# Squares moved behind the last products, weight casts and evacuations spread over later steps, and SP's transfers in written order, in a two-layer decoder trunk

## The chip, the cores and the metric

The kernel runs on one core of a Trainium2 chip. The core has a matrix engine (PE, with its weight loads listed as PEld), three engines for elementwise work (DVE, ACT, POOL) and a queue engine (SP) that issues transfers between HBM and the on-chip memory; here nearly all transfers are issued on SP. The metric is the device time of one execution in microseconds. The throttle on PE's clock is seen in the profile as the granted clock, 1.00 being full speed.

## The reference

The input x is 1024 positions by 1024 features, in float32. Two layers follow each other, each a token mixer and a feed-forward network with residual adds, with an RMS norm ahead of each part:

```
h = x
h = h + rg_lru_block(rms_norm(h, mix_norm[0]), ...)      # layer 0: recurrent mixer
h = h + swiglu_ffn(rms_norm(h, ffn_norm[0]), ...)        # d_ff = 2816
h = h + stick_breaking_attention(rms_norm(h, mix_norm[1]), w_qkv, w_o)   # layer 1, 16 heads of 64
h = h + swiglu_ffn(rms_norm(h, ffn_norm[1]), ...)
return rms_norm(h, final_norm)
```

The stick-breaking attention takes, for each query t and each earlier position s, sigmoid(z) at s times the product of sigmoid(-z) over the positions between s and t, where z is the scaled product of query and key; these weights multiply the values. The product of the sigmoids is a running product along the keys, so it is a scan.

## The kernel before

**Products.** Every float32 product is made of three matrix products in a reduced format (`mm3`, L140 to L143): the operands are split into a high and a low part, and high by high, high by low and low by high are added in PSUM. A split costs a cast (high part, usually on ACT) and a subtraction (low part, usually on DVE). Weights come as `raw` (a 128x1024 tile of 512 KB, `load_raw`, L114, from three buffers) and become `whi` and `wlo`. The activations are kept transposed: `h[d][n]` is the row block d of 8 (128 features) and the half n of 2 (512 positions); `xh[d][n]` and `xl[d][n]` are the two parts of h times the norm's gain. The normalising factor of each position is applied after the products, by a multiply with `rbc[n]`, so the products can begin before the statistics are known.

**End of layer 0.** The feed-forward network does its output product over 13 visits (`VISITS`), each for two row blocks d and d + 4, in seven products of halves (`ORDER`); in the last two visits rows 3, 7, 0 and 4 become final. When a row half has had its last add, `finished` (L1035) stores it (L1040, on SP), makes xh and xl (`prep`, L215 on ACT and L216 on DVE), and adds its square to the sum of squares (`squares`: L211 on ACT into a buffer, one for each n, L212 on DVE into `rbc[n]`). The weights of the first projection are loaded, cast and subtracted inside the last visit.

**Attention.** The program `qkv_steps(q)` makes, for the head pair q (0 to 7), the three projections Q, K and V (`which` 0, 1, 2), each in two halves n of eight `mm3` each over the rows k = 0 to 7, into one of two PSUM banks (`qk_ps`). It gives control back after each `mm3`, so a pair has 48 steps. At the start of each projection it loads the weights of the next one and casts them at once (`next_weights`: L1307, one 128x1024 cast on ACT); the two halves of the subtraction (L1309, DVE) are put into a list, `later`, of which the main loop takes one item a turn. At the end of a half the bank is evacuated: `t` (L1337, DVE, the multiply with `rbc[n]`), and in the same step, for Q and K, the cast `qh_` (L1346, ACT), the subtraction `ql_` (L1347, DVE) and the moves to the tiles that the scores read (L1348, on SP, 4 for a Q half and 8 for a K half); `qh_` and `ql_` have one buffer each, `t` has two. For V the half is transposed later (`v_turn`, `vt_ps`, put into a list `late`).

The main loop goes over 192 units of 16 heads. A turn does: the scores of a chunk (`z_part`, L1388 and L1389, PE, two PSUM banks `z_ps`); the transposes of weights two units ahead (`t_part`, L1426, PE) and their split `th`, `tl` (L1435 ACT, L1436 DVE); the two sigmoids of the scores, F (L1408) and w (L1409), on ACT, the scan over F (L1412 or L1414, DVE) and the multiply of w by F (L1415, POOL); one item of `later`; two steps of the fill, which is the projections of the next pair; and the product with the values (`av_part`, L1447, L1448). The scores run eight units ahead of the products with the values (`LEAD`). Before the loop, a prologue runs all 32 steps of Q and K of pair 0, with the statistics in between (`stats`: `st_ps` L201, `ms` L203, then a chain of small operations; `broadcast_r`: `rb_ps` L189, copied to `rbc`, L196), from the fifth step on.

After the last pair, the outputs of the heads, which had been stored to HBM in `od`, are brought back into xh and xl (L1495, L1496), the banks of the projections are closed, and the fill goes on with the output projection's first products (`ob`).

**What sets the order.** `tc.manual_schedule` keeps, on the engines it names, the order in which the program is written; operations of other engines are placed by the planner, which may issue a load long before the place where it is written. In the attention PE, ACT, DVE and POOL are named, SP is not. Each engine works through its instructions in order, so an instruction that waits holds up those behind it.

## Time and profile before

| | |
|---|---|
| time, median of three runs | 2208.43 us (2207.1 to 2210.01) |
| the profiled execution's own time | 2209.81 us |
| its span, first to last instruction | 2207.9 us |
| mean granted clock of PE | 0.994 |
| PE busy | 2176.5 us (99%) |
| DVE busy | 1709.9 us (77%) |
| ACT busy | 1150.2 us (52%) |
| load of attention weights, 512 KB, issue to landing | 3.8 us |

A line of the timeline gives the start of an instruction in us from the start of the span, its duration, the engine, the line of the kernel, the operation, what it writes and reads, and in brackets how long the engine sat idle before it and which engine's result ended that. A row with a count such as x8 is several instructions in a run. A waits line gives the engine and instruction that waited, what it waited for, the total, how often, and the longest. A busy PE is not a PE at its full clock: at clock 0.50 each matmul takes twice as long and still counts as busy.

### The profile page before, as it was taken

The numbers are of one execution on the slowest core, as the hardware profiler recorded it, in microseconds if no ns is written. First come the engines' busy times: TensorE is split into PE (matmuls) and PEld (weight loads), VectorE is DVE, ScalarE is ACT, GpSimd is POOL, SyncE is SP. The second block draws the span as 40 slices with busy tenths as digits, with TensorE's granted clock in tenths as the row PEclk, the third lists the DMA queues.
The fourth block names the chain that finished last, engine by engine and source line by source line (L and its number), as shares of the span: only waits on it lengthen the run. The fifth ranks groups of instructions, "written<-read, shape, count | busy, mean of one in ns | idle before, by whom it ended". The sixth has DMA issues, their size and how long they took to land.

```text
span 2207.9 us, 28478 instructions
## 1 busy us (share of the span) xinstructions
PE 2176.5 (99%) x10120; PEld 1805.7 (82%) x10120; DVE 1709.9 (77%) x2383; ACT 1150.2 (52%) x2007; POOL 287.2 (13%) x379
## 2 busy tenths in 40 slices
PE   7999999999999999999999999989999999999998
PEld 6888888888888888878888888878888888888887
DVE  6887778767777887878888888876876777788876
ACT  5577435343444544546666666653533444454556
POOL 2222020000000000003334333321000000000002
PEclk9999999999999999999999999989999999999999
DMA  7111412334444764444333333532133444467442
GB/s 230 48 48 39 134 39 72 102 123 158 143 149 134 261 209 122 148 136 98 89 94 96 105 87 104 177 128 70 39 110 124 148 148 133 154 225 234 137 152 86
DMA packets 298702, 277.72 MB, mean 126 GB/s; under 512 B 16312, under 2 KB 215104, under 8 KB 298560
## 3 DMA queue, kind: packets, MB, share of 16 engines
q1 hardware_dynamic: 298544, 275.91, 40.1%
q8 instruction: 79, 1.29, 0.2%
q14 instruction: 63, 0.52, 0.1%
q10 hardware_dynamic: 16, 0.00, 0.0%
HBM read 175.71 MB, written 74.97 MB: 114 GB/s over the span
## 4 chain that ended last, share of the span: by engine, by line
PE 88%; DVE 6%; ACT 3%; DMA 1%; issue 1%; SPq 1%; DVEq 0%; ACTq 0%
PE p_ps L143 18%; PE p_ps L141 18%; PE p_ps L142 18%; PE qk_ps L143 3%; PE qk_ps L141 3%; PE qk_ps L142 3%; PE wt_ps L1426 3%; PE ob_ps L142 2%; PE ob_ps L141 2%; PE ob_ps L143 2%; PE a_ps L143 2%; PE a_ps L142 2%; PE a_ps L141 2%; PE z_ps L1388 1%; DVE F L1414 1%; PE z_ps L1389 1%
## 5 line engine op out<-in xcount | busy, mean ns | idle before, releaser
L1415 POOL TENSOR_TENSOR w<-w,F 128x128 f32<-128x128 f32 (+1 forms) x192 | 183.7, 957 | 311.1 <-DVE F L1412 159.0
L143 PE MATMUL p_ps<-vh,wcl 128*128 128x512 f32 x524 | 204.2, 390 | 0.5 <-DVE wcl L682 0.5
L143 PE MATMUL p_ps<-vh,wbl 128*128 128x512 f32 x524 | 204.4, 390 | 0.3 <-DVE wbl L672 0.2
L143 PE MATMUL p_ps<-vh,wal 128*128 128x512 f32 x524 | 204.1, 389 | 0.1
L141 PE MATMUL p_ps<-vh,wbh 128*128 128x512 f32 x524 | 204.2, 390 | 0.0
L141 PE MATMUL p_ps<-vh,wch 128*128 128x512 f32 x524 | 204.1, 389 | 0.0
L142 PE MATMUL p_ps<-vl,wbh 128*128 128x512 f32 x524 | 203.9, 389 | 0.0
L142 PE MATMUL p_ps<-vl,wch 128*128 128x512 f32 x524 | 203.9, 389 | 0.0
L141 PE MATMUL p_ps<-vh,wah 128*128 128x512 f32 x524 | 203.9, 389 | 0.0
L142 PE MATMUL p_ps<-vl,wah 128*128 128x512 f32 x524 | 203.9, 389 | 0.0
L668 ACT CAST wbh<-sb 128x1024 fp32r<-128x1024 f32 (+2 forms) x69 | 69.6, 1009 | 193.7 <-DVE sb L652 193.6
L212 POOL TENSOR_TENSOR acc<-acc,rbc 128x512 f32<-128x512 f32 x30 | 40.4, 1348 | 773.6 <-ACT rbc L211 773.6
L1436 DVE TENSOR_TENSOR tl<-wt_ps,th 128x512 fp32r<-128x512 f32 x192 | 106.0, 552 | 39.2 <-ACT th L1435 37.1
L1435 ACT CAST th<-wt_ps 128x512 fp32r<-128x512 f32 x192 | 92.5, 482 | 83.1 <-PE wt_ps L1426 82.0
L141 PE MATMUL qk_ps<-vh,whi 128*128 128x512 f32 x264 | 118.6, 449 | 0.7 <-ACT vh L215 0.7
L143 PEld LDWEIGHTS p_ps<-vh,wbl 128*128 128x128 f32 x524 | 98.3, 188 | 22.3 <-DVE wbl L672 2.0
L143 PEld LDWEIGHTS p_ps<-vh,wcl 128*128 128x128 f32 x524 | 98.4, 188 | 21.9 <-DVE wcl L682 1.6
L143 PEld LDWEIGHTS p_ps<-vh,wal 128*128 128x128 f32 x524 | 98.4, 188 | 21.3 <-DVE wal L663 1.0
L142 PEld LDWEIGHTS p_ps<-vl,wah 128*128 128x128 f32 x524 | 98.4, 188 | 20.6
L142 PEld LDWEIGHTS p_ps<-vl,wch 128*128 128x128 f32 x524 | 98.4, 188 | 20.5
L142 PEld LDWEIGHTS p_ps<-vl,wbh 128*128 128x128 f32 x524 | 98.4, 188 | 20.5
L141 PEld LDWEIGHTS p_ps<-vh,wbh 128*128 128x128 f32 x524 | 98.4, 188 | 20.3 <-ACT ta L1053 0.2
(400 smaller groups left out, 5851.2 us busy)
## 6 DMA issues: line engine op xcount, KB each, us to landing
raw<-in_ffn_w_in SPq DMA_DIRECT2D x88, 512.0 KB, 3.8
vl<-pd SPq DMA_DIRECT2D x128, 256.0 KB, 3.6
pd<-U SPq DMA_DIRECT2D x90, 256.0 KB, 2.3
raw<-in_ffn_w_out SPq DMA_DIRECT2D x56, 256.0 KB, 3.9
raw<-in_attn_w_qkv SPq DMA_DIRECT2D x24, 512.0 KB, 3.8
raw<-in_lru_w_in SPq DMA_DIRECT2D x16, 512.0 KB, 4.1
acc<-pd SPq DMA_DIRECT2D x28, 256.0 KB, 2.6
pph<-rbc SPq DMA_DIRECT2D x28, 256.0 KB, 2.5
```

The lines of the kernel that those rows point to most:

```text
L141: nc.tensor.matmul(ps, lhsT=wh, rhs=mh, start=first, stop=False, **kw)
L142: nc.tensor.matmul(ps, lhsT=wh, rhs=ml, start=False, stop=False, **kw)
L143: nc.tensor.matmul(ps, lhsT=wl, rhs=mh, start=False, stop=last, **kw)
L212: (eng or nc.gpsimd).tensor_add(acc[n], acc[n], sq)
L668: nc.scalar.copy(self.full(self.wb), self.full(self.sb))
L1388: nc.tensor.matmul(ps[:, 0 : c1 - c0], lhsT=lhsT, rhs=KH[q][hx][:, c0:c1], start=True, stop=False)
L1389: nc.tensor.matmul(ps[:, 0 : c1 - c0], lhsT=lhsT, rhs=KL[q][hx][:, c0:c1], start=False, stop=True)
L1414: nc.vector.tensor_tensor_scan(rev, rev, rev, first, op0=ALU.mult, op1=ALU.bypass)
L1415: nc.gpsimd.tensor_mul(wt, wt, F[:, 1 : n + 1])
L1426: nc.tensor.transpose(tp[:, c : c + P], W[q, hx, j, kb // 4][:, (kb % 4) * P : (kb % 4 + 1) * P], ident)
L1435: nc.scalar.copy(th[:, q0:], tp[:, q0:])
L1436: nc.vector.tensor_sub(tl[:, q0:], tp[:, q0:], f32(th)[:, q0:])
```

## The change

- The squares of the four row blocks that become final in the last two visits (d = 0, 3, 4, 7, both halves) are left out of `finished`, and are done after the last products, first all of n = 0, then all of n = 1.
- `next_weights` does its work in three items of `later` in place of one cast at once and two items: the first half of the cast; the first half of the subtraction and the second half of the cast; the second half of the subtraction. Each is taken in a turn of its own.
- The first projection, Q of pair 0, takes its rows in the order 1, 5, 2, 6, 3, 7, 0, 4.
- The evacuation becomes a program of its own (`evacuate`): `t` is made in the step that ends the half, the rest (cast, subtraction, moves, or the entry of `v_turn` into `late`) a step later. For Q of pair 0 the whole of it is done at set places of the prologue.
- The prologue has 34 steps in place of 32; the statistics stand behind its steps 9 and 12, the broadcasts behind 14 and 18, the evacuations of Q behind 16 and 19 (`between`).
- The output's copies back from `od` are issued partly in V of the last pair (n = 0, pairs 0 to 5), the rest at the end; two empty steps before the first products of `ob` go.
- SP is named in the attention's `manual_schedule`, so the transfers are issued in the order written.

```diff
@@ -1029,7 +1029,8 @@
                     a, b = (ta, tb), GT[0] if final else held[0]
                 return dict(zip((0, 2, 3, 4), (*a, half(b, 0), half(b, 1))))
 
-            begun_sq = set()
+
+            begun_sq, last_sq = set(), []
             done = []
 
             def finished(d, n):
@@ -1039,7 +1040,10 @@
                 else:
                     nc.sync.dma_start(hd[d][n], h[d][n])
                     prep(h, d, n, gnext)
-                    squares(h, d, n, acc, rbc, V, first=n not in begun_sq)
+                    if d in (VISITS[-1][0], VISITS[-2][0], VISITS[-1][0] + HK, VISITS[-2][0] + HK):
+                        last_sq.append((d, n))
+                    else:
+                        squares(h, d, n, acc, rbc, V, first=n not in begun_sq)
                 begun_sq.add(n)
 
 
@@ -1196,6 +1200,8 @@
                         open_last()
             for dn in done:
                 finished(*dn)
+            for d, n in sorted(last_sq, key=lambda t: t[1]):
+                squares(h, d, n, acc, rbc, V, first=False)
             if final:
                 finish(h, nw, R, pp, (*GT, *UT))
         gs.close()
@@ -1300,21 +1306,29 @@
         wq = {(0, 0): wq0[0]}
 
 
-        late, later = [], []
+        late, later, waiting = [], [], []
+
+        def bring_back(*which):
+            for q, n in which:
+                nc.sync.dma_start(f32(xh[q][n]), od[q, n][0])
+                nc.sync.dma_start(f32(xl[q][n]), od[q, n][1])
 
         def next_weights(raw):
             hi, lo = wtile("whi"), wtile("wlo")
-            nc.scalar.copy(hi, raw)
-            for i in range(NH):
-                later.append(lambda c=half(hi, i), a=half(lo, i), b=half(raw, i): nc.vector.tensor_sub(a, b, f32(c)))
+            part_hi = lambda i: nc.scalar.copy(half(hi, i), half(raw, i))
+            part_lo = lambda i: nc.vector.tensor_sub(half(lo, i), half(raw, i), f32(half(hi, i)))
+
+            def second():
+                part_lo(0)
+                part_hi(1)
+
+            later.extend((lambda: part_hi(0), second, lambda: part_lo(1)))
             k3 = lambda t: t.rearrange("p (k c) -> p k c", k=ND)
             return k3(hi), k3(lo)
 
 
 
         def qkv_steps(q):
-            full = lambda tag: [ap.tile([P, S], F32R, tag=tag, name=tag, bufs=4) for _ in range(2)]
-            VV[q] = ap.tile([P, NT, 2, P], F32R, tag="v", name="v", bufs=2)
             for which in range(3):
                 w = wq.pop((q, which))
                 nx = (q, which + 1) if which < 2 else (q + 1, 0)
@@ -1325,51 +1339,67 @@
                     mix[0].w[mix[0].order[0]] = next_weights(mix[0].raw.pop(0))
                     mix[0].load(1)
                     mix[0].load(2)
+
+                ks = (1, 5, 2, 6, 3, 7, 0, 4) if (q, which) == (0, 0) else range(ND)
                 for n in range(NH):
                     ps = psQ.tile([P, NB], F32, tag="qk", name="qk_ps")
-                    for k in range(ND):
-                        mm3(ps, w[0][:, k], w[1][:, k], xh[k][n], xl[k][n], k == 0, k == ND - 1)
-                        if k == 3 and late:
+                    for i, k in enumerate(ks):
+                        mm3(ps, w[0][:, k], w[1][:, k], xh[k][n], xl[k][n], i == 0, i == ND - 1)
+                        if i == 3 and late:
                             late.pop()()
-                        if k < ND - 1:
+                        if i < ND - 1:
                             yield
-                    t = ap.tile([P, NB], F32, tag="t", name="t", bufs=2)
-                    nc.vector.tensor_mul(t, ps, rbc[n])
-                    cs = slice(n * NB, (n + 1) * NB)
-                    if which == 0 and n == 0:
-                        Q[q] = full("q")
-                    if which == 1 and n == 0:
-                        KH[q], KL[q] = full("kh"), full("kl")
-                    if which < 2:
-                        th = ap.tile([P, NB], F32R, tag="qh_", name="qh_", bufs=1)
-                        tl = ap.tile([P, NB], F32R, tag="ql_", name="ql_", bufs=1)
-                        nc.scalar.copy(th, t)
-                        nc.vector.tensor_sub(tl, t, f32(th))
-                        move = lambda dst, p0, src, p1: nc.sync.dma_start(f32(dst)[p0, cs], f32(src)[p1])
-                        for hx, (a, b) in enumerate(((top, bot), (bot, top))):
-                            if which == 0:
-                                move(Q[q][hx], a, th, a)
-                                move(Q[q][hx], b, tl, a)
-                            else:
-                                for dst, src in ((KH[q][hx], th), (KL[q][hx], tl)):
-                                    move(dst, top, src, a)
-                                    move(dst, bot, src, a)
+                    ev = evacuate(q, which, n, ps)
+                    if (q, which) == (0, 0):
+                        waiting.append(ev)
+                        yield
                     else:
-
-                        def v_turn(n=n, t=t):
-                            tp = psQ.tile([P, NB], F32, tag="qk", name="vt_ps")
-                            for i in range(4):
-                                nc.tensor.transpose(tp[:, i * P : (i + 1) * P], t[:, i * P : (i + 1) * P], ident)
-                            src = tp.rearrange("p (b h c) -> p b h c", b=4, h=2)
-                            bs = slice(4 * n, 4 * n + 4)
-                            for hx in range(2):
-                                nc.scalar.copy(VV[q][:, bs, hx, 0:HD], src[:, :, hx])
-                                nc.vector.tensor_sub(
-                                    VV[q][:, bs, hx, HD:P], src[:, :, hx], f32(VV[q])[:, bs, hx, 0:HD]
-                                )
-
-                        late.append(v_turn)
-                    yield
+                        next(ev)
+                        yield
+                        next(ev, None)
+
+
+        def evacuate(q, which, n, ps):
+            full = lambda tag: [ap.tile([P, S], F32R, tag=tag, name=tag, bufs=4) for _ in range(2)]
+            t = ap.tile([P, NB], F32, tag="t", name="t", bufs=2)
+            nc.vector.tensor_mul(t, ps, rbc[n])
+            yield
+            cs = slice(n * NB, (n + 1) * NB)
+            if which == 0 and n == 0:
+                Q[q] = full("q")
+            if which == 1 and n == 0:
+                KH[q], KL[q] = full("kh"), full("kl")
+            if which < 2:
+                th = ap.tile([P, NB], F32R, tag="qh_", name="qh_", bufs=1)
+                tl = ap.tile([P, NB], F32R, tag="ql_", name="ql_", bufs=1)
+                nc.scalar.copy(th, t)
+                nc.vector.tensor_sub(tl, t, f32(th))
+                move = lambda dst, p0, src, p1: nc.sync.dma_start(f32(dst)[p0, cs], f32(src)[p1])
+                for hx, (a, b) in enumerate(((top, bot), (bot, top))):
+                    if which == 0:
+                        move(Q[q][hx], a, th, a)
+                        move(Q[q][hx], b, tl, a)
+                    else:
+                        for dst, src in ((KH[q][hx], th), (KL[q][hx], tl)):
+                            move(dst, top, src, a)
+                            move(dst, bot, src, a)
+                return
+            if n == 0:
+                VV[q] = ap.tile([P, NT, 2, P], F32R, tag="v", name="v", bufs=2)
+
+            def v_turn():
+                tp = psQ.tile([P, NB], F32, tag="qk", name="vt_ps")
+                for i in range(4):
+                    nc.tensor.transpose(tp[:, i * P : (i + 1) * P], t[:, i * P : (i + 1) * P], ident)
+                src = tp.rearrange("p (b h c) -> p b h c", b=4, h=2)
+                bs = slice(4 * n, 4 * n + 4)
+                for hx in range(2):
+                    nc.scalar.copy(VV[q][:, bs, hx, 0:HD], src[:, :, hx])
+                    nc.vector.tensor_sub(VV[q][:, bs, hx, HD:P], src[:, :, hx], f32(VV[q])[:, bs, hx, 0:HD])
+
+            late.append(v_turn)
+            if q == NP - 1 and n == 0:
+                bring_back(*((p, 0) for p in range(NP - 2)))
 
 
         W = {}
@@ -1478,22 +1508,11 @@
         units = [u for q, hx in heads for u in unit_list(q, hx)]
         LEAD = 8
 
-
-        def stats_steps():
-            for n in range(NH):
-                stats(rbc[n], psO, "o", n)
-                for _ in range(ND - (1 if n else 6)):
-                    yield
-                broadcast_r(psO, "o", n)
-                yield
-
         def all_fill():
             yield from first
             for q in range(1, NP):
                 yield from qkv_steps(q)
-            for q, n in od:
-                nc.sync.dma_start(f32(xh[q][n]), od[q, n][0])
-                nc.sync.dma_start(f32(xl[q][n]), od[q, n][1])
+            bring_back((NP - 2, 0), *((p, 1) for p in range(NP - 2)))
             yield
             yield
             late.pop()()
@@ -1502,8 +1521,6 @@
             po = pos.enter_context(tc.tile_pool(name="fpo", bufs=1, space=PSUM, side="right", reuse_waits="tile"))
             ob = po.tile([P, S], F32, name="ob")
             mix.append(ob)
-            for _ in range(2):
-                yield
             for i, d in enumerate(mix[0].order[:2]):
                 w = mix[0].w[d]
                 for k in range(ND - 1):
@@ -1514,15 +1531,23 @@
         fill = all_fill()
         ready = {}
         E = mybir.EngineType
-        with tc.manual_schedule(engines={E.PE, E.Activation, E.DVE, E.Pool}):
-            sts, first = stats_steps(), qkv_steps(0)
-
-
-            for i in range(2 * ND * NH):
-                if i >= 5:
-                    next(sts, None)
+        with tc.manual_schedule(engines={E.PE, E.Activation, E.DVE, E.Pool, E.SP}):
+
+
+            first = qkv_steps(0)
+            between = {
+                9: lambda: stats(rbc[0], psO, "o", 0),
+                12: lambda: stats(rbc[1], psO, "o", 1),
+                14: lambda: broadcast_r(psO, "o", 0),
+                16: lambda: [*waiting[0]],
+                18: lambda: broadcast_r(psO, "o", 1),
+                19: lambda: [*waiting[1]],
+            }
+            for i in range(1, 2 * ND * NH + 3):
                 next(first)
-                if i >= 5 and later:
+                if i in between:
+                    between[i]()
+                if i > 4 and later:
                     later.pop(0)()
             for u in range(-LEAD, len(units)):
                 c = u + LEAD
```

## The prediction

> **What bounds the kernel now.** I read the page first (busy shares, chain), then the waits of PE and of the queue SP, then two stretches in the timeline: the end of layer 0 with the start of attention, and one period of attention.
>
> ```profile
> span 2207.9 us, 28478 instructions
> PE 2176.5 (99%) x10120; PEld 1805.7 (82%) x10120; DVE 1709.9 (77%) x2383; ACT 1150.2 (52%) x2007; POOL 287.2 (13%) x379
> raw<-in_attn_w_qkv SPq DMA_DIRECT2D x24, 512.0 KB, 3.8
> ```
>
> ```profile
> PE ob L141 <- issue: 3.9, 1, 3.9
> PE z_ps L1388 <- ACT w L1409: 2.5, 7, 0.4
> ```
>
> ```profile
> SPq L114 <- DVE wlo L1309: 104.3, 22, 17.5
> ```
>
> PE is busy 99% of the span, so a gain can only be idle PE time or time at half clock, and any new PE wait is paid in full. In the waits (total, times, longest), the largest single idle stretch of attention is the 3.9 us before `ob`; the waits of z for ACT come to 2.5 us over seven times. The third fence matters most: loads of the attention weights (L114) wait 104.3 us for a free buffer (released by `wlo`). They run as far ahead as three buffers allow, and land (3.8 us) long before their cast.
>
> **End of layer 0** (start, duration, engine; the bracket is the idle time before and what ended it):
>
> ```profile
> 923.83 0.39 PE L143 MATMUL p_ps<-vh,wcl 128*128 128x512 f32 x1
> ...
> 925.87 0.39 PE L143 MATMUL p_ps<-vh,wal 128*128 128x512 f32 x1
> ...
> 959.27 0.50 PE L143 MATMUL p_ps<-vh,wcl 128*128 128x512 f32 x1 [0.53 <-DVE wcl L682]
> 962.26 0.50 PE L141 MATMUL p_ps<-vh,wd 128*128 128x512 f32 x1 [0.42 <-ACT ta L1053]
> 968.77 0.51 PE L141 MATMUL qk_ps<-vh,whi 128*128 128x512 f32 x1 [0.66 <-ACT vh L215]
> 969.95 0.50 PE L142 MATMUL qk_ps<-vl,whi 128*128 128x512 f32 x1 [0.67 <-DVE vl L216]
> ```
>
> ```profile
> 968.00:971.30 3.30, 1.98 (x11) 1.24 (x10) 2.49 (x4) 2.53 (x4) 0.17 (x1) 1.00 0.70 240
> 971.30:974.70 3.40, 3.40 (x11) 2.82 (x11) 2.20 (x8) 0.20 (x1) 0.52 (x3) 0.50 0.00 0
> 1439.80:1445.70 5.90, 5.90 (x20) 5.02 (x21) 4.67 (x5) 3.51 (x9) 1.09 (x1) 0.50 0.71 202
> ```
>
> In the second fence (length, PE busy, PEld, DVE, ACT, POOL, granted clock), PE was idle 3.30 − 1.98 = 1.3 us up to 971.30, and the next 3.40 us ran at clock 0.50, a loss of 1.7 us. After the 3.91 us of `ob`, 5.9 us ran at 0.50: 3.0 us lost.
>
> Moving the last eight squares behind the products frees ACT and DVE for the work that PE waits for, and the new row order (rows finished early first) hides `prep`. Undisturbed matmuls of this size start every 0.227 us (nine starts from 923.83 to 925.87). The four waits show 0.53 + 0.42 + 0.66 + 0.67 = 2.3 us of idle time; by the starts around them against 0.227 each, they lost 0.80 + 0.70 + 0.82 + 1.05 = 3.4. With the 1.7 of half clock: −5.1 us.
>
> What becomes late is the statistics, which need the squares:
>
> ```profile
> 965.03 0.62 ACT L211 ACTIVATE acc<-h 128x512 f32<-128x512 f32 x1
> 969.80 0.68 DVE L212 TENSOR_TENSOR rbc<-rbc,acc 128x512 f32<-128x512 f32 x1
> 970.54 1.18 PE L201 MATMUL st_ps<-ones,rbc 128*128 128x1 f32 x8
> ```
>
> The squares of one half share one buffer, so each takes ACT 0.62, then DVE 0.68, and some 0.07 of handover: 1.38 us. Four of n = 0 take 5.5 us after the last `prep`. `st_ps` of n = 0 stands behind nine products (0.68 us each, three matmuls of 0.227), which started while `prep` of the last rows was still to do: by hand it waits 1.75 us, the second one 2.55 (three products cover 2.0 of a chain that ends 4.6 later), and the second projection 0.25 for the scale. Added: 4.55 us, and half clock between nothing and one stretch of 3.4 us; I take the 1.7 lost in the row above. Net +1.1 us (−5.1 if the new waits are all covered, to +2.9).
>
> **Start of attention.** SP's order is now the written one: the load of the third weights stands behind the four moves of the first Q half, and each evacuation's rest comes one step later.
>
> ```profile
> 976.38 0.69 DVE L1337 TENSOR_TENSOR t<-qk_ps,rbc 128x512 f32<-128x512 f32 x1
> 977.84 0.53 SPq L1348 DMA_DIRECT2D q<-qh__7618  x1
> 979.69 0.59 SPq L1348 DMA_DIRECT2D q<-ql__7619  x1
> 990.46 1.10 SPq L1348 DMA_DIRECT2D kh<-qh__7720  x2
> 994.70 0.36 PE L1389 MATMUL z_ps<-kl,q 128*128 128x256 f32 x1
> 995.97 0.62 ACT L1346 CAST qh__7759<-t 128x512 fp32r<-128x512 f32 x1 [5.53 <-DMA kh<-qh__7720]
> 996.61 1.28 ACT L1408 ACT_TABLE_LOAD   x1
> 998.40 0.44 PE L1388 MATMUL z_ps<-kh,q 128*128 128x384 f32 x1 [0.32 <-ACT w L1409]
> ```
>
> Count from the end of the first `t` (T). First move at T + 0.8 (977.84 − 977.07), fourth done at T + 3.2; the load issues at 3.3, lands at 7.1 (3.8). DVE's order is `wlo` of these weights before the second `t`: half a `whi` (0.53, see 1112.21 to 1112.74 below), half a `wlo` (0.66), `t` (0.69): T + 9.04. The second K half's products, needing that bank, were ready at T + 6.5: a stall of 2.55 us. `th` has one buffer, and waits for the DMA that reads it (5.53 in the row): second Q half moved at T + 9.8 to 12.25, its readers landed at 13.45, first K half moved from 14.1; z(0) needs the first of these landed, 4.2 us later as before (990.46 to 994.70): T + 18.3, while PE gets there at 15.9: 2.35 us. `th` of the second K half follows 5.5 us after the first move (990.46 to 995.97): 19.6; its eight moves end 5.6 later (0.65 from `th` to the first, as 1112.21 to 1112.86 below, and 4.96, as 1112.86 to 1117.82): 25.1. Only then is the first load of pair 1 issued; landed 28.95; two halves of cast 30.1; the table load, which stood before that cast, now stands behind it: 31.4; F and w of z(0): 31.9. z(2) needs that, and PE is ready at 21.75: 10.15 us. Sum 15.05, less the z waits of this place (0.8), plus half clock after the long stall (3.4 to 6.8 us of it: 2.5 lost) and after the two others (1.7): +18.5 us (12 to 21).
>
> **Each later pair.** One period is 60.4 us for 24 steps of the loop, two projection steps each. The rows around the second Q half and the second K half of pair 1:
>
> ```profile
> 1089.71 0.61 ACT L1409 ACTIVATE w<-z_ps 128x512 f32<-128x512 f32 x1
> 1094.05 0.61 ACT L1435 CAST th<-wt_ps 128x512 fp32r<-128x512 f32 x1
> 1094.81 0.41 ACT L1409 ACTIVATE w<-z_ps 128x256 f32<-128x256 f32 x1
> 1109.77 0.60 ACT L1409 ACTIVATE w<-z_ps 128x512 f32<-128x512 f32 x1
> 1112.21 0.62 ACT L1346 CAST qh__9181<-t 128x512 fp32r<-128x512 f32 x1 [1.84 <-DVE t L1337]
> 1112.74 0.37 ACT L1435 CAST th<-wt_ps 128x256 fp32r<-128x256 f32 x1
> 1115.03 0.26 ACT L1435 CAST th<-wt_ps 128x128 fp32r<-128x128 f32 x1
> 1115.46 0.39 ACT L1409 ACTIVATE w<-z_ps 128x256 f32<-128x256 f32 x1
> ```
>
> ```profile
> 1092.43 0.46 SPq L1348 DMA_DIRECT2D q<-qh__8931  x1
> 1094.32 0.59 SPq L1348 DMA_DIRECT2D q<-ql__8932  x1
> 1112.86 1.10 SPq L1348 DMA_DIRECT2D kh<-qh__9181  x2
> 1116.57 1.25 SPq L1348 DMA_DIRECT2D kl<-ql__9182  x2
> ```
>
> ```profile
> 1097.84 0.39 PE L1388 MATMUL z_ps<-kh,q 128*128 128x512 f32 x1
> 1117.03 0.39 PE L1388 MATMUL z_ps<-kh,q 128*128 128x512 f32 x1
> ```
>
> The delayed rest is a gain: ACT need not sit 1.84 us for `t`, and six of the seven z waits on w (some 0.5 us each with the drain) go, one a pair. But the load behind a rest is now issued after that rest's moves, and its cast stands on ACT one loop step later, ahead of the next `th`, F and w. K case: the half's cast starts when the last w ends (1110.37), eight moves run 1111.05 to 1116.1 (as long as 1112.86 to 1117.82), the load lands at 1119.9. ACT reaches that of the weights at 1111.6 (1110.37, that half's 0.53 and 0.7 for `th`, F and w of the next step) and stands until then, two z buffers and `th` two units ahead cover some steps, then PE stops: cast 0.53, then `th`, F and w (0.82, from 1115.03 to 1115.85) give 1121.25 for the z wanted at 1117.03: 4.2 us. Q case: the cast of the half starts at 1090.3 (1089.71 + 0.60), four moves 1090.95 to 1093.4, landed 1097.3; 0.53 and 1.17 (`th` to the end of w, 1094.05 to 1095.22) give 1099.0 for the z wanted at 1097.84: 1.2 us. The third load of a pair stands behind no move and runs ahead. Half clock after 4.2 us of stall is priced by the nearest row, 3.91 us of idle: 3.0 lost (0 to 3.4); after 1.2 us by 1.3 us idle followed by 1.7, against the seven waits of 0.4 us followed by none: 0.5 (0 to 1.7). A pair costs 4.2 + 1.2 + 3.0 + 0.5 − 0.5 = +8.4; seven pairs (the last one's K case waits for the first weights of `w_o` in the same way): +58.6 (25 to 73).
>
> **End of attention.** The two empty steps before `ob` go and the copies back to `xh` for n = 0 are issued earlier, so `vt_ps` and `ob` come back to back; but `ob` takes the banks that V's copies read, and waits for these as now: nothing, +1 for one more unit behind the fill where DVE is late (−4 to +2).
>
> Sum: 1.1 + 18.5 + 58.6 + 1 = +79 on the profiled run's 2209.81 (span 2207.9 and 1.9 around it), 2289; that run stands 1.4 over the median of 2208.43, so 2287.5.
>
> [...]
>
> **Rivals.**
> [...] Chance 0.17.
> (2) The loads of the pairs are covered: z's two buffers, `th` two units ahead and ACT (52% busy) catch up. For it: 5.4 us of slack between 1111.6 and 1117.03. Against: the load needs 8.3. It decides at 5.4 us from ACT's arrival to landing, that is, if the moves are issued in 2 us in place of 5. Then only the start pays: 1 + 18.5 + 1 − 3.7 = +17: 2225. Chance 0.13.
> (3) Faster: SP's loads are not late anywhere, since the moves' data come earlier by the whole delay of a rest; then −5.1 at the end of layer 0, −0.8 at z(2), −3.7 in the pairs and 2 of the 4.55 added: 2208 − 8 = 2200. It decides when the load of pair 1 lands before z(2) is wanted, 10 us sooner than my chain. Chance 0.05.
> (4) Worse: DVE (77%), idle while ACT stands, does not catch up after ACT's stop and PE stops a second time for `tl`, 2 to 4 us a pair: 2300 to 2315. Chance 0.12.
> (5) The loads keep their lead and the squares take back what the waits give: same. Chance 0.04.
>
> **Numbers.** The forecast itself (2268 to 2300) has 0.49. The range goes from 2222, just under the time of (2), to 2310: it holds 0.49, 0.17, some 0.10 of (2) and 0.07 of (4). About 0.2% (4.4 us) is what can be told from no change: faster 0.05, same 0.04, slower 0.91.
>
> **What would show it.** In the changed kernel: some 14 waits of `whi` on ACT for the DMA of `raw`, 3 to 8 us each; PE waits of z for w of about 4 us once and 1 us once a period; about 68 us a period; clock below 1 some 3 to 7 us after each; no waits for `vh` and `vl` at 968. If `raw` on SP still lies a projection ahead of its moves, or ACT's casts don't wait, the prediction is wrong.

## The result and the profile after

The changed kernel takes 2302.09 us (median of four runs, 2296.0 to 2303.02), the kernel before beside it 2208.98 us. The ratio is 1.042 (95% interval 1.040 to 1.044): 93 us slower. The forecast was 2287 us, within 2222 to 2310; the time lies just above the forecast's own band of 2268 to 2300.

The page of the kernel after: span, busy shares, and the chain of work that ended last, by engine.

```profile
span 2300.9 us, 28495 instructions
PE 2204.2 (96%) x10120; PEld 1823.5 (79%) x10120; DVE 1713.2 (74%) x2383; ACT 1154.0 (50%) x2031; POOL 295.2 (13%) x379
PE 83%; DVE 6%; DMA 4%; ACT 3%; SPq 2%; issue 2%; DVEq 0%; ACTq 0%
```

PE executes the same 10120 instructions, but is now idle 4% of the span, and DMA stands on the chain with 4%. The waits of the kernel after (total, times, longest) name the place:

```profile
ACT whi L1318 <- DMA raw<-in_attn_w_qkv: 111.1, 15, 9.9
PE z_ps L1418 <- ACT w L1439: 60.4, 15, 11.2
ACT whi L1318 <- DMA raw<-in_attn_w_o: 9.1, 1, 9.1
PE ob L141 <- issue: 5.2, 1, 5.2
```

ACT stands 16 times, 7.5 us on average, at the cast of weights that have not landed. PE waits 15 times for the w that is queued on ACT behind such a cast. In the kernel before that wait of PE came to 2.5 us.

I cut both traces at the same four pieces of work: the first product of the first projection, the first projection product of pair 1, the last projection product, and the last product with the values. The windows of the kernel before, then of the kernel after (from, to, length, then PE busy, PEld, DVE, ACT, POOL, and the granted clock):

```profile
963.75:1010.70 46.95, 45.17 (x215) 36.57 (x213) 29.05 (x51) 19.45 (x37) 6.62 (x17) 0.96 0.50 129
1010.70:1431.61 420.91, 418.70 (x2237) 352.24 (x2236) 355.57 (x516) 278.01 (x677) 166.10 (x280) 1.00 0.38 103
1431.61:1478.78 47.17, 40.55 (x200) 33.48 (x199) 38.03 (x50) 29.80 (x73) 16.41 (x25) 0.86 0.31 105
```

```profile
960.42:1029.69 69.27, 51.11 (x211) 40.34 (x209) 30.20 (x54) 21.88 (x43) 5.72 (x15) 0.83 0.31 80
1029.69:1520.86 491.17, 439.71 (x2233) 365.87 (x2232) 357.82 (x516) 280.88 (x698) 171.14 (x280) 0.95 0.34 91
1520.86:1571.47 50.61, 41.58 (x208) 33.92 (x206) 40.91 (x52) 31.02 (x76) 20.18 (x27) 0.87 0.24 84
```

| stretch | before | after | difference | forecast |
|---|---|---|---|---|
| up to the first projection | 963.75 | 960.42 | −3.3 | in the next row |
| to the projections of pair 1 | 46.95 | 69.27 | +22.3; with the row above +19.0 | +1.1 + 18.5 = +19.6 |
| seven pairs | 420.91 | 491.17 | +70.3 | +58.6 |
| to the last product with the values | 47.17 | 50.61 | +3.4 | +1 |
| the rest | 729.12 | 729.43 | +0.3 | 0 |
| span | 2207.9 | 2300.9 | +93.0 | +79 |

Of the first row, 1.3 us are no part of the change: a product that both kernels reach at 620 us, far ahead of the edits, starts that much earlier in this execution (619.65 for 620.97). In the seven pairs, PE's busy time grew by 21.0 us at the same products. After the stalls PE works 37.0 us at clock 0.50 there. In this trace its 128x512 matmuls start every 0.43 us at clock 0.50 and every 0.23 us at 1.00, 1.9 times as far apart and not twice, so half clock is 17 to 18.5 us of it (18.5 counts half of the time at 0.50 as lost, as the sums below do); the rest was not told apart. The other 49.3 us are idle time.

One K case of the kernel after, in the projections of pair 2, in the timeline (the rows that the prediction gives to pair 1 are of pair 2 as well: its projections begin at 1070.48 in the kernel before):

```profile
1144.78 1.10 SPq L1377 DMA_DIRECT2D kh<-qh__9188  x2
1148.93 1.24 SPq L1377 DMA_DIRECT2D kl<-ql__9189  x2
1150.21 0.58 SPq L114 DMA_DIRECT2D raw<-in_attn_w_qkv  x1
```

```profile
1154.25 0.62 ACT L1318 CAST whi<-raw 128x512 fp32r<-128x512 f32 x1 [8.88 <-DMA raw<-in_attn_w_qkv]
```

```profile
1130.68 0.50 PE L1418 MATMUL z_ps<-kh,q 128*128 128x512 f32 x1 [1.38 <-ACT w L1439]
1155.64 0.80 PE L1418 MATMUL z_ps<-kh,q 128*128 128x512 f32 x1 [5.40 <-ACT w L1439]
```

The eight moves take SP from 1144.78 to 1150.17; only then is the load issued. It lands 4.0 us later, and ACT has stood 8.88 us. The first PE row is the Q case of the same pair (1.38 us), the second the K case (5.40 us).

### The profile page after: what moved, and what is told of

Same layout as the page of the kernel before. It is cut to its first block, busy times and chain, and to the rows that moved or that the text cites. A ratio compares the mean times of both kernels' runs of the same rounds, so it can differ in the third digit from the quotient of the medians.

```text
span 2300.9 us, 28495 instructions
## 1 busy us (share of the span) xinstructions
PE 2204.2 (96%) x10120; PEld 1823.5 (79%) x10120; DVE 1713.2 (74%) x2383; ACT 1154.0 (50%) x2031; POOL 295.2 (13%) x379
## 4 chain that ended last, share of the span: by engine, by line
PE 83%; DVE 6%; DMA 4%; ACT 3%; SPq 2%; issue 2%; DVEq 0%; ACTq 0%
PE p_ps L143 17%; PE p_ps L141 17%; PE p_ps L142 17%; DMA raw<-in_attn_w_qkv 3%; PE ob_ps L142 2%; PE ob_ps L141 2%; PE ob_ps L143 2%; PE qk_ps L141 2%; PE a_ps L142 2%; PE a_ps L141 2%; PE a_ps L143 2%; PE qk_ps L143 2%; PE qk_ps L142 2%; PE wt_ps L1456 2%; SPq L1377 2%
## 5 line engine op out<-in xcount | busy, mean ns | idle before, releaser
L1445 POOL TENSOR_TENSOR w<-w,F 128x128 f32<-128x128 f32 (+1 forms) x192 | 191.6, 998 | 390.7 <-DVE F L1442 222.8
L1418 PE MATMUL z_ps<-kh,q 128*128 128x256 f32 (+1 forms) x192 | 73.6, 383 | 61.1 <-ACT w L1439 60.4
L1442 DVE TENSOR_TENSOR_SCAN F<-F,unit 128x128 f32<-128x128 f32 (+3 forms) x128 | 113.0, 883 | 3.0 <-ACT F L1438 3.0
L141 PEld LDWEIGHTS p_ps<-vh,wch 128*128 128x128 f32 x524 | 98.3, 188 | 20.5 <-ACT tb L1057 0.2
```

Source lines behind the costliest of these rows:

```text
L141: nc.tensor.matmul(ps, lhsT=wh, rhs=mh, start=first, stop=False, **kw)
L1418: nc.tensor.matmul(ps[:, 0 : c1 - c0], lhsT=lhsT, rhs=KH[q][hx][:, c0:c1], start=True, stop=False)
L1442: nc.vector.tensor_tensor_scan(rev, rev, unit[:, NB - n :][:, ::-1], first, op0=ALU.mult, op1=ALU.add)
L1445: nc.gpsimd.tensor_mul(wt, wt, F[:, 1 : n + 1])
```

## The experiments

Theory: the loads of the attention weights lost their lead, since SP keeps the written order and each load is written behind the moves of an evacuation; ACT, in order, stands at the cast, and F and w behind it starve PE. Rival: the later rest of an evacuation and the cast in three items cost by their places on ACT and DVE. Ratios are to the kernel before, on the same chip.

### SP out of the written order

```diff
-        with tc.manual_schedule(engines={E.PE, E.Activation, E.DVE, E.Pool, E.SP}):
+        with tc.manual_schedule(engines={E.PE, E.Activation, E.DVE, E.Pool}):
```

> The changed kernel with SP taken out of the engines whose written order is kept in the attention; all else of the change stays. Theory (the loads of the attention weights are issued behind the moves of an evacuation, and ACT, in order, stands at their cast): the loads run ahead again, the fourteen stalls of the pairs (about 10 us a pair, 70 in all) and some 14 of the 18.5 us at the start of attention go: 2202 to 2220 us, waits of whi for raw near nothing. Rival (the later rest of the evacuation and the halved casts cost by their places on ACT and DVE): 2280 to 2302, with z still waiting for w 4 to 6 us once a pair.

Measured: 2214.51 us, ratio 1.0029 (1.0018 to 1.0040). Its waits have none of `whi` for `raw` left, and PE waits for w once:

```profile
PE z_ps L1418 <- ACT w L1439: 1.1, 1, 1.1
```

A pair takes 60.54 us (1071.52 to 1132.06). Of the 93 us, about 87 go with this one word, as the theory said; the other parts of the change together still cost 6 us.

### The one word in the kernel before

The same list of engines, in the kernel before, with SP added and nothing else.

> The kernel before with one word added: SP named among the engines in written order. Theory: the loads lose their lead as in the changed kernel, and the cast, which here follows the load at once and whole, stands on ACT even earlier: K stalls of about 6.7 us and Q stalls of 3.4 with half clock behind both, 13 to 16 us a pair, and 15 to 20 at the start: 2310 to 2340 us. Rival (naming SP changes little, the rest of the change costs): 2205 to 2215.

Measured: 2325.71 us, ratio 1.0527 (1.0509 to 1.0544). The waits of that kernel:

```profile
ACT whi L1307 <- DMA raw<-in_attn_w_qkv: 103.2, 15, 8.7
PE z_ps L1388 <- ACT w L1409: 79.5, 23, 7.8
```

From the projections of pair 2 to those of pair 3 (1099.97 to 1175.23) a pair takes 75.3 us, 14.9 more than before. The K stalls there are 6.3 to 7.8 us and the Q stalls 2.9 to 3.9, as expected. So naming SP makes the loss without the rest of the change, and a larger one. That the changed kernel's later cast in two halves saves the difference fits, but no run shows it alone.

### The load written ahead of the moves

```diff
+                while rest:
+                    next(rest.pop(0), None)
...
                         next(ev)
-                        yield
-                        next(ev, None)
+                        if n == 0 or (q, which) == (NP - 1, 2):
+                            yield
+                            next(ev, None)
+                        else:
+                            rest.append(ev)
+                            yield
...
-                16: lambda: [*waiting[0]],
+                17: lambda: [*waiting[0]],
```

The first two lines stand behind the load, at the start of a projection.

> The changed kernel, SP in written order, but the load at the start of a projection is written ahead of the rest of the evacuation before it (so ahead of that half's 4 or 8 moves), and Q's first evacuation of pair 0 comes one prologue step later, behind the load. The casts stay where they are. Theory: the 8 moves of the second K half (5.4 us) no longer stand between, the load lands before ACT reaches its cast: pairs back to about 60 us each, start of attention 4 to 8 us over that of before in place of 18.5: 2204 to 2222 us. Rival (it is the cast one turn after the load that is too early, whatever stands ahead on SP: 4 us of landing against 2.5 us of a turn): stalls of 1 to 2 us a projection stay, 2225 to 2250.

Measured: 2221.22 us, ratio 1.0057 (1.0042 to 1.0072), at the upper end of the expected range. SP stays in written order, the casts stay where they are, and a pair takes 60.57 us (1075.61 to 1136.18). The moves between were the cause. What remains is one wait each at the start, as forecast:

```profile
ACT whi L1318 <- DMA raw<-in_attn_w_qkv: 3.5, 1, 3.5
PE z_ps L1423 <- ACT w L1444: 5.1, 1, 5.1
```

### The loads written a projection earlier

```diff
+        loads = [(q, x) for q in range(NP) for x in range(3)][1:]
+
+        def load_next():
+            if loads:
+                q, x = loads.pop(0)
+                raws[q, x] = load_raw(cols(w_qkv, x * D + q * P), (ND,))
...
-                    wq[nx] = next_weights(load_raw(cols(w_qkv, nx[1] * D + nx[0] * P), (ND,)))
+                    if (q, which) == (0, 0):
+                        load_next()
+                    load_next()
+                    wq[nx] = next_weights(raws.pop(nx))
```

> The changed kernel, SP in written order, each load written one projection earlier (two ahead of its use). Theory: loads land some 15 us before their cast, as in the kernel before: 2200 to 2215 us, no wait of whi for raw, z waits of the pairs gone (also the 0.4 us ones of before). Rival (places on ACT and DVE): 2280 to 2302.

Measured: 2220.4 us, ratio 1.0057 (1.0042 to 1.0072), above the expected range. The loads of the attention weights are early, a pair takes 60.55 us (1070.32 to 1130.87), but the first load of `w_o` was not moved and still stands behind the last eight moves:

```profile
ACT whi L1324 <- DMA raw<-in_attn_w_o: 8.3, 1, 8.3
PE z_ps L1427 <- ACT w L1448: 5.5, 2, 4.1
```

So a single load left in the written place costs a z wait of 4.1 us.

### The casts one turn later

```diff
-            later.extend((lambda: part_hi(0), second, lambda: part_lo(1)))
+            later.extend((*[lambda: None] * turns[0], lambda: part_hi(0), second, lambda: part_lo(1)))
...
+            turns[0] = 1
             for u in range(-LEAD, len(units)):
```

`turns` starts as `[0]`, so the extra turn begins with the main loop.

> The changed kernel as it is (SP in written order, loads behind the moves), but from pair 1 on the weight casts come one turn of the loop (about 2.5 us) later. Theory (ACT, in order, stands at the cast until the load has landed, and z's two banks cover 3.4 us of it): the 5.4 us stall of a pair falls to about 2.9, the one of 1.4 us goes, the start of attention stays: 2262 to 2282 us. Rival (what counts is when the load lands, not where ACT meets it): 2294 to 2304.

Measured: 2306.18 us, ratio 1.0448 (1.0434 to 1.0462): my number was wrong, and the time lies just above the rival's range too. The waits, and the K case of pair 2, show why it does not decide between them:

```profile
ACT whi L1318 <- DMA raw<-in_attn_w_qkv: 90.5, 15, 9.6
PE z_ps L1418 <- ACT w L1439: 44.1, 8, 11.1
PE av_ps L1477 <- DVE oo L1488: 17.8, 6, 3.1
...
1155.54 0.58 PE L1418 MATMUL z_ps<-kh,q 128*128 128x256 f32 x1 [4.29 <-ACT w L1439]
```

The Q stalls went (8 waits of z in place of 15) and the K stalls shrank by 1.1 us (5.40 to 4.29), not 2.5; ACT goes through the extra turn, of small tiles, in 0.84 us (1144.63 to 1145.47). But the subtractions `wlo`, a turn later too, now fall together with those of a Q half on DVE, and `av_ps` waits 3 us for `oo`, six times; behind the wait that ends at 1112 the clock was 0.65 over 4.9 us (1112.1 to 1117). A cast can't be moved without the work that goes with it; the dose I wanted was not given.

### The last squares back in their place

```diff
-                    if d in (VISITS[-1][0], VISITS[-2][0], VISITS[-1][0] + HK, VISITS[-2][0] + HK):
-                        last_sq.append((d, n))
-                    else:
-                        squares(h, d, n, acc, rbc, V, first=n not in begun_sq)
+                    squares(h, d, n, acc, rbc, V, first=n not in begun_sq)
```

This and the next runs have SP out of the written order; their base is 2214.51 us.

> The kernel with SP out of the written order (2214.5 us), and the last eight squares back in the place where their row becomes final. The row order of the first projection and the prologue's places stay. By the prediction's sum for the end of layer 0 (some 5 us of waits removed, some 6 added at the statistics) the two nearly cancel: 2211 to 2216 us, with the first st_ps no longer waiting 2.8 us. Rival (the move itself is a gain, the prologue's other parts lose it): 2217 to 2220. Rival (the move is the loss): 2208 to 2210.

Measured: 2209.18 us, ratio 1.0007 (0.9998 to 1.0016). The second rival holds: moving the squares is a loss, of about 5 us. Rows of the kernel with the squares moved (SP out of the written order), then of this one:

```profile
972.54 1.87 PE L201 MATMUL st_ps<-ones,rbc 128*128 128x1 f32 x8 [2.61 <-DVE rbc L212]
961.92:1012.10 50.18, 46.11 (x210) 37.14 (x209) 30.05 (x54) 21.78 (x43) 5.71 (x15) 0.93 0.46 123
```

```profile
970.18 0.95 PE L201 MATMUL st_ps<-ones,rbc 128*128 128x1 f32 x8
962.66:1006.77 44.11, 42.70 (x211) 34.88 (x210) 26.73 (x49) 18.38 (x37) 5.71 (x15) 1.00 0.52 138
```

The stretch from the first projection to pair 1 is 44.11 in place of 50.18 us: no wait of `st_ps` for the squares, and no half clock (1.00 for 0.93). It is also 2.8 us shorter than before (46.95); one turn of z and transposes, under 1 us, has moved out of it by the two more prologue steps. In the trace of the kernel before with six empty steps (the last run below), whose code up to here is that of the kernel before, the stretch is 45.65 us (961.95 to 1007.60), and the granted clock of the whole execution is 0.997, against 0.994 before. So the rest of the change at this place is a gain of between 0.5 and 2 us. The row order is the part of it that touches the first products; it was not run alone.

### The two empty steps before ob

```diff
             mix.append(ob)
+            for _ in range(2):
+                yield
```

> The kernel with SP out of the written order (2214.5 us), and the two empty steps before the first products of ob back. Theory (the step removed from the fill makes PE stand 5.2 us in place of 3.9 at ob): ob's wait back to about 3.9 us, 2212 to 2213.5 us. Rival (the tail is bound by DVE, so PE stands elsewhere for the same time): 2214 to 2215.5, ob's wait shorter and the waits for tl longer.

Measured: 2213.27 us, ratio 1.0028 (1.0016 to 1.0040); `ob` waits 4.2 us, not 5.2. That agrees with the theory, but 1.2 us is within what the intervals allow, and by the ratios (1.0028 for 1.0029) nothing is left of it: the time doesn't show it.

### The rest of an evacuation in the step of t

```diff
                         next(ev)
-                        yield
                         next(ev, None)
+                        yield
```

> The kernel with SP out of the written order (2214.5 us), and the rest of each evacuation back in the step that ends the half (from pair 0's K on). By the prediction (ACT then stands for t, one z wait of some 0.5 us a pair returns): 2217 to 2219 us. Rival (a pair takes 60.5 us either way, since another wait of 0.5 us takes the place of the z wait): 2213 to 2216.

Measured: 2224.9 us, ratio 1.0082 (1.0068 to 1.0096), above both ranges. What returns is not the z wait but a wait on DVE (its waits, and the window of one pair):

```profile
PE av_ps L1477 <- DVE oo L1488: 10.6, 6, 1.8
...
1069.30:1131.29 61.99, 60.23 (x323) 50.44 (x322) 52.44 (x75) 40.36 (x100) 25.54 (x41) 1.00 0.35 94
```

A pair takes 61.99 us in place of 60.54: beside the cast in three items the later rest is worth 1.4 us a pair, three times what I had put. Six waits of `av_ps` take 1.8 us each. The one of this pair, 1.76 us, left the clock at 1.00; over the whole execution it is 0.993, against 0.995 in the base.

### The cast whole and at once

```diff
-            later.extend((lambda: part_hi(0), second, lambda: part_lo(1)))
+            nc.scalar.copy(hi, raw)
+            later.extend((lambda: part_lo(0), lambda: part_lo(1)))
```

The base is the kernel with the squares back (2209.18 us).

> SP out of the written order, the squares back (2209.2 us), and the weights cast whole, at once, at the start of a projection as in the kernel before (the rest of an evacuation stays a step later). If the three-item cast is worth something by itself, a pair gets longer than 60.5 us: 2212 to 2220. If it only spreads work that has room, a pair stays at 60.4 to 60.6: 2207 to 2211.

Measured: 2206.41 us, ratio 0.9996 (0.9987 to 1.0004), below both ranges. Windows of one pair, in the kernel with the squares back and in this one:

```profile
1066.18:1126.72 60.54, 60.16 (x323) 50.54 (x322) 50.50 (x75) 40.71 (x100) 24.39 (x41) 1.00 0.36 97
```

```profile
1066.68:1126.65 59.97, 59.97 (x323) 50.55 (x321) 50.92 (x75) 40.10 (x97) 25.90 (x41) 1.00 0.37 97
```

With the later rest and the cast at once, PE is never idle in a pair: 59.97 us, against 60.40 before. The cast in three items costs 0.6 us a pair, when the loads are early. The traces carry this; the times alone (2206.41 for 2209.18) have intervals that meet.

### More empty steps before ob

Six, then ten empty steps, on the kernel with the squares back, which has none there; and six in the kernel before, whose edit is shown.

```diff
             mix.append(ob)
-            for _ in range(2):
+            for _ in range(6):
                 yield
```

> SP out of the written order, the squares back (2209.2 us), and six empty steps before the first products of ob in place of none. Theory (PE stands at ob for the copies of V, which wait on ACT and DVE; the fill has spare steps at the end, so more turns of z and transposes before ob fill the wait): ob's wait from 5.2 to under 2 us, part of the 3 us of half clock behind it goes: 2202 to 2206 us. Rival (the tail is bound by DVE, the steps only move the idle time): 2207 to 2210.

> As the one before, with ten empty steps. Theory (PE's wait at ob): no wait left at ob, no half clock there, the stalls for tl at the very end shorter since products still lie between them: 2200 to 2205 us. Rival (DVE bound): 2207 to 2211, with the waits for tl longer.

> The kernel before with six empty steps before the first products of ob in place of two, nothing else. Theory (PE's wait at ob): its 3.9 us shrinks to about 1, part of the half clock behind it goes: 2202 to 2206 us. Rival (DVE bound): 2206 to 2209.

Measured: 2205.79 us (0.9991, 0.9982 to 1.0000), 2205.71 us (0.9991, 0.9982 to 0.9999) and 2204.37 us (0.9987, 0.9979 to 0.9996). The first and the last lie in the theory's ranges, the one with ten steps between the theory's range and the rival's. The last is 2.7 us faster than the kernel before (2207.02 beside it), a difference at the edge of what these runs can tell. The wait moved rather than went, in all three: no wait of `ob` is left, but PE now stands at a z (4.14, 4.15 and 3.87 us). In the kernel before with six steps, that is behind the copies of V and a cast of 1.05 us on ACT:

```profile
1438.71 0.48 PE L1388 MATMUL z_ps<-kh,q 128*128 128x256 f32 x1 [3.87 <-ACT w L1409]
1428.11:1471.05 42.94, 36.73 (x199) 30.19 (x198) 38.59 (x50) 30.02 (x73) 18.97 (x27) 0.96 0.35 119
```

The stretch is 42.94 us in place of 47.17, with clock 0.96 in place of 0.86: the idle time at `ob` is nearly the same (3.87 for 3.91), half clock is less, and `ob`'s products now lie between the waits for `tl` at the end (1.3 us in all).

## Why the prediction was right, and where its sizes were off

**The side and the mechanism.** Right: the loads behind the moves, ACT standing at the cast, z two banks later. Run on its own, the one word costs 117 us in the kernel before and gives some 87 back in the changed one. Rivals (2) and (3), loads covered, fell: (2) put the cover at 5.4 us from ACT's arrival to the landing; ACT waited 8.88, and PE stood for 5.40 of it, so the cover is 3.5. The 5.4 left out the work that still stands ahead of the z after the landing (first half of the cast, `th`, F and w: 1.4 us here). The time itself lies in the band of rival (4), 2300 to 2315, but not by its mechanism: PE waits for `tl` three times (3.8 us in all), never in the seven pairs. What brought it there are longer stalls.

**Each pair: +8.4 forecast, +10.0 measured (70.3 over seven).** This is the term that was mis-sized, on both sides. The stalls were too small: over the seven pairs K stalls are 5.5 us on average (4.4 to 6.5), not 4.2, and Q stalls 1.5 (1.0 to 2.3), not 1.2. In the pair shown above the moves took 5.4 us and not 5.0 and the load 4.0 us and not 3.8, and PE reached the blocked z 5.5 us after the first move, not 6.0. The clock was put a little too high. The windows ahead of and behind the Q stall of that pair, behind its K stall, and around the Q stall of pair 4:

```profile
1127.00:1130.60 3.60, 2.30 (x12) 1.59 (x10) 0.50 (x1) 1.63 (x5) 0.00 (x0) 1.00 0.35 106
1130.60:1134.00 3.40, 3.32 (x16) 2.69 (x17) 3.40 (x7) 3.15 (x8) 1.33 (x3) 1.00 0.02 5
...
1155.60:1159.00 3.40, 3.36 (x10) 2.77 (x11) 3.40 (x6) 3.00 (x7) 1.61 (x3) 0.50 0.00 0
1159.00:1162.50 3.50, 3.50 (x22) 3.07 (x22) 3.44 (x6) 2.46 (x6) 1.65 (x4) 0.99 0.00 0
...
1268.30:1271.71 3.41, 1.14 (x6) 0.62 (x5) 0.75 (x2) 1.89 (x5) 0.00 (x0) 1.00 0.02 7
1271.71:1275.13 3.42, 3.42 (x10) 2.71 (x11) 3.42 (x6) 3.01 (x7) 1.61 (x3) 0.50 0.00 0
```

After 1.3 us of idle time the clock stays at 1.00; after the K stall of 5.4 us it is 0.50 for another 3.4 us. Behind the other K stalls that lasted 3.4 to 6.1 us. Of the seven Q stalls only the longest, 2.27 us in pair 4, was followed by 0.50, for 3.4 us. PE's busy time grew by 21.0 us over seven pairs: 3.0 a pair, where I had put 3.5. The 0.17 for no half clock after the stalls of the pairs was wrong for every K stall and for one Q stall, right for six.

The length of a stall alone does not tell which way it goes. In the same trace the Q stall of 1.95 us in pair 6 left the clock at 1.00, and so did the wait of 2.58 us for `t` at the start of attention, longer than the 2.27 us of pair 4. What decides was not shown.

**The gain of the later rest.** I put −0.5 a pair, for a z wait that goes. It goes, and pairs with early loads still take 60.54 us, since waits of `av_ps` for `oo` on DVE (0.4 us) take its place. The cast at once shows the gain (59.97 for 60.40 before, −0.4): the mechanism was right, and the step that failed was that the cast in three items costs nothing when loads are early.

**Start of attention: +18.5.** For the end of layer 0 and the start together 19.0 was measured, 20.3 without the 1.3 us from far ahead, where 19.6 was forecast. The stalls of the start came one by one:

```profile
993.12 0.50 PE L141 MATMUL qk_ps<-vh,whi 128*128 128x512 f32 x1 [2.58 <-DVE t L1365]
1000.99 0.35 PE L1418 MATMUL z_ps<-kh,q 128*128 128x256 f32 x1 [0.73 <-DMA kh<-qh__7721]
1002.31 0.35 PE L1419 MATMUL z_ps<-kl,q 128*128 128x256 f32 x1 [0.97 <-DMA kl<-ql__7722]
1016.81 0.69 PE L1418 MATMUL z_ps<-kh,q 128*128 128x384 f32 x1 [11.16 <-ACT w L1439]
```

2.58 for 2.55; 0.73 + 0.97 for 2.35; 11.16 for 10.15. The long stall left 5.7 us of work at 0.50 (1016.81 to 1022.54), 2.9 us lost where 2.5 was put; after the other two the clock stayed at 1.00, where 1.7 was put.

**End of layer 0: +1.1, some 2.7 by the rows, and wrong in what it joined.** I gave the waits of `vh` and `vl` and their half clock (3.6 us) to the moved squares and the row order together. With the squares back these waits do not return: the row order, not the squares, removed them, as far as these runs tell. The squares' move alone saves 2.0 us ahead of the first projection (two waits of products, 0.54 and 0.42 us, and what is lost around them) and costs some 6 behind it, 2.61 of it the wait of `st_ps`, the rest mostly half clock. In the kernel after, the window up to 971.34 has PE busy 0.80 us, and the next 10.2 us ran at 0.50, 5.1 us lost where 1.7 was put:

```profile
967.93:971.34 3.41, 0.80 (x6) 0.38 (x4) 2.02 (x4) 1.78 (x3) 0.00 (x0) 1.00 0.00 0
971.34:981.58 10.24, 10.24 (x33) 8.36 (x33) 4.03 (x16) 3.47 (x6) 0.69 (x3) 0.50 0.01 2
```

The first `st_ps` waited 2.61 us where 1.75 was put. The second, with 2.55, did not wait in this trace, where PE came to it at half clock; in five of the experiments it waits, 0.7 to 1.1 us (both waits of `st_ps` come to 3.3 to 3.7 us there, 2.6 of it the first). By these rows the place costs 2.6 + 5.1 and saves 2.0, 1.3 (the waits of `vh` and `vl`) and 1.7 (their half clock), about +2.7.

**End of attention: +1 forecast, +3.4 measured.** `ob` waits 5.2 us in place of 3.9, and the waits for `tl` at the end are longer. One turn more lies in this stretch, for which I had put the 1. With SP out of the written order it is 50.4 us (1433.38 to 1483.77), and with the two empty steps back 48.3 (1432.88 to 1481.15). So in these traces the steps that I took as nothing are worth 2 us, 1.0 of it at `ob`; the times of the two runs do not show it.

**What stays open.** Rival (4), a second stop for DVE, is not seen as a wait of its own in the changed kernel; how much of the longer K stall is DVE's backlog was not told apart. Nor was it shown why 1.3 us of idle time (waits of 0.66 and 0.67 us) was followed by 3.4 us at 0.50 in the kernel before, near 970, and a Q stall of 1.38 us in the kernel after by 1.00.

## What to carry to other kernels

When an issuing queue is put into written order, a load gets the place of its line: behind every move written ahead of it (eight here, 5.4 us), and those moves wait for computed data. Look for the in-order engine that consumes the load, and compare the time from its arrival there to the landing (8.9 us here) with what the buffers behind it cover (3.5 us here). Write such loads ahead of the moves, or a stage earlier, and test each part of a compound change alone: here one word cost 117 us in the kernel before, and in the changed kernel it hid a small gain of the later evacuation (0.4 us a pair with the cast at once) and a loss of some 5 us by the squares' move.

## What the runs showed of the hardware that was not expected

- Stalls of like length were followed by different clocks. In the kernel after, 3.4 us at 0.50 came behind a stall of 2.27 us (pair 4), while the clock stayed at 1.00 behind stalls of 1.95 us (pair 6) and 2.58 us (the wait for `t` at 993). In the kernel before, two waits of 0.66 and 0.67 us near 970 were followed by 3.4 us at 0.50. So what a short stall costs could not be read from its length here.
- Medians over the first pairs, from issue to landing of a 512 KB load: 3.8 us (3.6 to 4.0, seven loads) with SP out of the written order, 4.1 us (3.8 to 4.6, six loads) in the kernel after, and 5.1 us (3.9 to 5.3, seven loads) in the kernel with the load ahead of the moves. What makes the last longer was not told apart.
